# A two-layer hybrid decoder trunk: each engine's instruction order taken from a list schedule over the traced program

## The chip, the cores and the metric

The kernel runs on one core of one Trainium2 chip. A core has five engines that work side by side, each through its own queue of instructions: TensorE (PE) multiplies matrices and loads weights for it (PEld), VectorE (DVE) and ScalarE (ACT) work element by element, GpSimd (POOL) does a little elementwise work here, and SyncE (SP) issues the transfers between the chip's memory and the core's on-chip memory. Engines wait for one another through semaphores. The metric is the device time of one execution in microseconds (us), from the first to the last instruction and what lies around it; lower is better.

## The reference

One sequence of 256 tokens with 2048 features goes through two layers. Both modulate their input with adaLN, and end in a post-norm residual. Layer A is a Mamba-2 mixer (64 heads in 8 groups, one chunk of 256 tokens), layer B attends with three dilated windows to keys and values made from layer A's output. Cut to what matters:

```python
def reference(x, c, ada_w, ada_b, ln_g, ln_b, a_in_w, ..., kv_w, b_in_w, b_out_w):
    for layer in range(DEPTH):                                    # DEPTH = 2
        shift, scale, gate = _adaln(c, ada_w[layer], ada_b[layer])  # silu(c) @ w + b
        h = x * (1.0 + scale) + shift
        if layer < N_A_LAYERS:
            y = _ssd_mixer(h, ...)       # h @ in_w, conv, SiLU, chunked scan, gate, norm, @ out_w
        else:
            y = _dilated_mixer(h, k_sh, v_sh, b_in_w[0], b_out_w[0])
        x = _layer_norm(DEEPNORM_ALPHA * x + (1.0 + gate) * y, ln_g[layer], ln_b[layer])
        if layer == N_A_LAYERS - 1:
            k_sh, v_sh = _shared_kv(x, kv_w)
    return x
```

All inputs and the output are 32-bit floats.

## The kernel before

**Weights.** Every large weight comes in pieces of 512 KB, 128 partitions by 1024 columns. `load_piece` (line 85) issues the load into one of six buffers called `raw`. `split` (line 90) makes two tiles out of it: ScalarE rounds it to `whi` (line 93), VectorE subtracts to get the remainder `wlo` (line 95); there are four buffers of each. A product of two 32-bit matrices is then three matmuls in the faster format: high by high, high by low, low by high. `cm_piece` (lines 119 to 121) does it with the weights as the stationary operand and 256 tokens moving, `cm_wide` (151 and 152) with both parts of the activation in one matmul of 512 columns, `tm_mults` (172 to 174) with the activation stationary and 512 weight columns moving. Activations lie in the tile `actT`, split in the same manner.

**adaLN.** The modulation of 2048 features is a vector by matrix product. It runs on VectorE: `ada_dot` (line 237) multiplies a tile `araw` of 1 MB (128 outputs by 2048 inputs, loaded by `ada_load` at line 230) with `silu(c)` in `cb_` and sums along the row. There are 96 such dots: 32 for shift and scale of layer 0, 16 for its gate, 48 for layer 1. The last two groups are background work: `queue` and `background` put one in after every few pieces. `gate_out` (line 244) transposes a finished gate and writes it out.

**Stages.** (1) The first matmuls (line 425) spread `c` over all partitions, ScalarE takes its SiLU (426), VectorE makes two dots, and ScalarE and VectorE the first tile of `h` (384 to 386). While the other tiles of `h` come, TensorE works on pieces of ten different products, in an order that is written out by hand (lines 395 to 398): each product is begun on the tiles of `h` that exist, and its part sum is put aside (483 and 485). (2) For eight groups `product` makes `bc`, `xs` and `z`, `conv` does the convolution (303 to 308), `stage1`, `stage2` and `stage3` the scan of a group (L551 and L553 make decay factors, L562 transposes, L541 evicts scores, L592 and L584 multiply, L594 gates). (3) `y_tiles` transposes and splits the result (645 to 648), four chunks of the output projection follow, each with `residual` (663 to 665). (4) `ln_scale` computes the LayerNorm's factors in a chain of some fifteen small VectorE operations that ends in `nb` (677); lines 700 and 702 apply them in column chunks, block 0 on ScalarE, block 1 on VectorE; `x_tiles` transposes (715) and splits (718 to 720). (5) Keys and values, layer B's queries, attention (`attend`) and gate. (6) The last projection; its second half keeps all pieces split in memory, so that token block 0 ends before block 1, and block 0's norm and output (882 to 885) run beside block 1's matmuls.

**What sets the order.** Each engine executes its queue in order. The kernel is written with a framework that traces the program in Python, then gives each engine its queue, places tiles in buffers and adds the semaphores; of what is ready in its own simulation it takes what was traced first. Besides, a few places are pinned by hand: a list cell `pin[0]` and the `after` arguments hold an instruction, and `tc.issue_after(ins)` makes the instructions traced in its block come behind `ins` in their engine's queue. Dots are pinned behind the first h steps (line 436), behind the last split before group 1 (609) and before the wide key products (745); the splits after the LayerNorm are pinned behind `nb` (740 and 746).

Of the kernel before, what the change touches and what calls it, by code (L numbers as in the profile page):

```python
# [49 lines left out]
def trunk(ctx, tc, xT, x, c, par, cst, bias, lnrow, ada, wdt, win, wout, wkv, wk1, wbin, wbout, out):  # L50
# [38 lines left out]

    def split(raw, into=None, after=None):  # L90

        hi, lo = into or [wp.tile([P, 1024], F32R, name=n, bufs=4) for n in ("whi", "wlo")]
        S.activation(hi, raw, AF.Copy)  # L93
        with tc.issue_after(after) if after is not None else ExitStack():
            latest[0] = V.tensor_tensor(lo, raw, hi.bitcast(F32), op=ALU.subtract)  # L95
        return hi.rearrange("p (k n) -> p k n", k=2), lo.rearrange("p (k n) -> p k n", k=2)

    jobs, latest, pin = [], [None], [None]

# [8 lines left out]

    def cm_piece(src, q, ps, ahi, alo, k0=0, k1=KT, raw=None, after=None):


        hi, lo = split(load_piece(src[q]) if raw is None else raw, after=after)
        for k in range(2):
            kt = 2 * q + k
            for n in range(4):
                o = ps[n // 2][:, n % 2, :]
                c_ = slice(n * P, n * P + P)
                first = kt == k0 and n % 2 == 0
                T.matmul(o, hi[:, k, c_], ahi[:, kt, :], start=first, stop=False, skip_group_check=True)  # L119
                T.matmul(o, hi[:, k, c_], alo[:, kt, :], start=False, stop=False, skip_group_check=True)  # L120
                T.matmul(o, lo[:, k, c_], ahi[:, kt, :], start=False, stop=kt == k1 - 1, skip_group_check=True)  # L121

    def cm_quads(work, ahi, alo, pre=None, after=None):
        for q in range(KT // 2):
            if pre:
                pre(q)
            for src, ps in work:
                cm_piece(src, q, ps, ahi, alo, after=after if q == 0 else None)

# [103 lines left out]
    def ada_dot(layer, kind, ct, raw):  # L233

        j = KIND.index(kind)
        with tc.issue_after(pin[0]) if pin[0] is not None else ExitStack():
            V.scalar_tensor_tensor(raw, raw, 1.0, cb_, op0=ALU.mult, op1=ALU.mult,  # L237
                                   accum_out=mod[layer][:, ct, j:j + 1])

# [33 lines left out]
    with ExitStack() as cA:  # L273
# [14 lines left out]
        with ExitStack() as cS:  # L288
# [63 lines left out]
            with ExitStack() as c0:  # L352
# [15 lines left out]
                def h_step():  # L368
# [6 lines left out]
                    ada_dot(0, kind, kt, raw)  # L375
                    if kt > 1:
                        pin[0] = None
                    fetch()
# [53 lines left out]
                for _ in range(2):  # L432
                    for _ in range(2):
                        h_step()
                    while late:
                        pin[0] = late.pop()().ins
                    fetch_piece()
# [169 lines left out]
            for g in range(G - 1):  # L607
                if g == 1:
                    pin[0] = latest[0].ins
                    queue(wp1, [(0, "gate", kt) for kt in range(KT)])  # L610
                    jobs.append(lambda: gate_out(0))
                if g % 2 == 1:
                    product("bc", g + 1)
                product("xs", g + 1)
                if rs is not None:
                    stage3(g - 1, rs)
                st1 = stage1(g)
                if g < G - 2:
                    product("z", g + 1)
                rs = stage2(g, *st1)  # L620
# [46 lines left out]
        def ln_scale(blocks=(0, 1)):  # L667
# [8 lines left out]
            nb = sm.tile([P, n], F32, name=tag + "nb", bufs=1)  # L676
            last = V.scalar_tensor_tensor(nb, mv[:, :, 0], -1.0, r, op0=ALU.mult, op1=ALU.mult)
            return r, nb, last

# [14 lines left out]
        drain()  # L694
        r, nb, nb_last = ln_scale()
        for c0_, c1_ in ((0, 256), (256, 512), (512, 1024), (1024, 1536), (1536, 2048)):
# [39 lines left out]
    with ExitStack() as cL:  # L736
        pl = cL.enter_context(tc.tile_pool(name="pl", bufs=3))
        ex = cL.enter_context(tc.tile_pool(name="ex1", bufs=2, space=PSUM))
        ps = [acc_pair(), acc_pair(), acc_pair(ex)]
        cm_quads([(wkv[2 * g], ps[g]) for g in range(NG)], xhi, xlo, pre=ahead, after=nb_last.ins)  # L740
        for g in range(NG):
            evict_k(0, g, ps[g])

        R = (4, 9)
        pin[0] = latest[0].ins
        with tc.issue_after(nb_last.ins):
            queue(pl, cols1[16:])
            jobs.append(lambda: gate_out(1))
            for g in range(NG):
                for w in range(2):  # L750
                    cm_wide(wk1[2 * g + w], kk[1][:, g, 2 * w:2 * w + 2, :], rate=R)
            for hq in range(2):
                for g in range(NG):
                    ps = tm_chunk(wkv[6 + 2 * g + hq], hx, lx, rate=R)
                    for b in range(2):
                        S.activation(vt[hq][:, g, b, :], ps[b], AF.Copy)
            drain()

# [115 lines left out]
    for b in range(2):  # L874
        for n in range(2):
            for q in range(4):
                tm_mults(q, held[4 * n + q], ps[n], *og, 0, H, (b,))
            join(2 + n, ps[n][b], b)
        r, nb, _ = ln_scale((b,))
        for c in range(4):  # L880
# [3 lines left out]
            V.tensor_tensor(u[b][:, cs_], u[b][:, cs_], lnt[:, 1, cs_], op=ALU.add)  # L884
            nc.sync.dma_start(out[b * P:b * P + P, cs_], u[b][:, cs_])


# [85 lines left out]
```

## Time and profile before

| | |
|---|---|
| runs without the profiler | 1299.74 us median of 3, 1298.78 to 1300.66 |
| profiled execution, its span from first to last instruction | 1298.3 us |
| mean granted TensorE clock in it | 0.989 of full speed |
| moved by DMA | 334.82 MB, mean 258 GB/s |
| matmuls, weight loads | 7386 each |

The profile records one execution; its own time is the span of 1298.3 us, which is 1.4 us under the median of the runs. Its page gives each engine's busy time, then groups of equal instructions: line, engine, operation, output and input tiles, count, busy time, mean duration in ns, and the idle time of the engine before them with what ended it. Other views list who waited for whom, the instructions in order of time, and busy time, clock and DMA share by stretch. A busy TensorE is not yet one at its peak, since a matmul's end is modelled and overlaps the next. Times in the views count from the span's start.

### The profile page before, as it was taken

Reading aid. Unit: us, or ns where it says so; the run is one execution under the profiler, and the core shown is the slowest. Engines: PE = TensorE matmul, PEld = TensorE weight load, DVE = VectorE, ACT = ScalarE, POOL = GpSimd, SP = SyncE. Lnnn points to the kernel's source line nnn. Section 1 sums busy time; section 2 is a strip of 40 time slices with the busy share of each in tenths; the row PEclk is TensorE's granted clock in tenths of the full one; section 3 lists DMA queues with packets and bytes.
Section 4 is the critical chain, followed back from the end, with each engine's and each line's share of the span. In section 5 each row is a group of like instructions: output and inputs, shape, how many; then the busy total and the mean of one; then the engine's idle time right before and its main releaser. Section 6 shows DMA issues by size and latency. Waiting matters only on the chain.

```text
span 1298.3 us, 19349 instructions
## 1 busy us (share of the span) xinstructions
PE 1249.2 (96%) x7386; PEld 1097.9 (85%) x7386; DVE 1029.1 (79%) x1457; ACT 709.1 (55%) x1039; POOL 27.6 (2%) x20
## 2 busy tenths in 40 slices
PE   6999999999999999999999799999999999999995
PEld 4878988899899999778888699888887888888884
DVE  5888887899999778899765578888768747758687
ACT  3544457867687687864333444444435645445651
POOL 0000000000000000000000043000000000000000
PEclk9999999999999999999999899999999999999998
DMA  9999966697885546398977575999897754352461
GB/s 373 407 374 408 384 203 239 221 343 239 305 315 180 183 160 211 132 336 325 386 254 219 190 238 175 352 380 368 326 345 276 268 181 145 114 188 89 163 259 65
DMA packets 80449, 334.82 MB, mean 258 GB/s; under 512 B 9090, under 2 KB 9314, under 8 KB 67684
## 3 DMA queue, kind: packets, MB, share of 16 engines
q1 hardware_dynamic: 80356, 333.58, 71.2%
q8 instruction: 58, 0.95, 0.3%
q14 instruction: 35, 0.29, 0.1%
HBM read 331.37 MB, written 2.18 MB: 257 GB/s over the span
## 4 chain that ended last, share of the span: by engine, by line
PE 86%; DVE 9%; ACT 3%; issue 2%; DMA 1%; SPq 0%; DVEq 0%; ACTq 0%
PE acc L151 13%; PE acc L173 12%; PE acc L174 11%; PE acc L172 11%; PE acc L121 9%; PE acc L119 8%; PE acc L120 8%; PE acc L152 6%; DVE wlo L95 2%; DVE araw L237 2%; PE py L592 2%; PE aux L801 1%; ACT whi L93 1%; PE po L815 1%; PE po L825 1%
## 5 line engine op out<-in xcount | busy, mean ns | idle before, releaser
L95 DVE TENSOR_TENSOR wlo<-raw,whi 128x1024 fp32r<-128x1024 f32 x395 | 486.0, 1243 | 189.7 <-ACT whi L93 187.5
L93 ACT ACTIVATE whi<-raw 128x1024 fp32r<-128x1024 f32 x395 | 412.6, 1056 | 326.9 <-PE acc L174 141.6
L119 PE MATMUL acc<-actT,whi 128*128 128x256 f32 x960 | 274.9, 289 | 14.0 <-ACT actT L385 8.9
L173 PE MATMUL acc<-wlo,actT 128*128 128x512 f32 x704 | 276.7, 393 | 3.2 <-DVE wlo L95 3.1
L121 PE MATMUL acc<-actT,wlo 128*128 128x256 f32 x960 | 271.9, 287 | 4.5 <-DVE wlo L95 4.5
L120 PE MATMUL acc<-actT,whi 128*128 128x256 f32 x960 | 273.9, 287 | 0.0
L172 PE MATMUL acc<-whi,actT 128*128 128x512 f32 x704 | 272.2, 394 | 0.8 <-ACT actT L647 0.7
L151 PE MATMUL acc<-actT,whi 128*128 128x512 f32 x704 | 250.8, 398 | 0.0
L237 DVE SCALAR_TENSOR_TENSOR araw<-araw,cb__72 128x2048 f32<-128x2048 f32 x96 | 219.2, 2285 | 17.9 <-ACT cb__72 L426 9.2
L119 PEld LDWEIGHTS acc<-actT,whi 128*128 128x128 f32 x960 | 187.2, 196 | 17.8 <-ACT actT L385 10.6
L152 PE MATMUL acc<-actT,wlo 128*128 128x256 f32 x704 | 201.4, 286 | 0.0
L121 PEld LDWEIGHTS acc<-actT,wlo 128*128 128x128 f32 x960 | 185.9, 195 | 6.5 <-DVE wlo L95 6.4
L120 PEld LDWEIGHTS acc<-actT,whi 128*128 128x128 f32 x960 | 187.7, 195 | 0.3
L174 PE MATMUL acc<-whi,actT 128*128 128x512 f32 x448 | 175.0, 391 | 0.0
L173 PEld LDWEIGHTS acc<-wlo,actT 128*128 128x128 f32 x704 | 132.3, 188 | 33.4 <-DVE wlo L95 6.9
L151 PEld LDWEIGHTS acc<-actT,whi 128*128 128x128 f32 x704 | 132.3, 188 | 30.2
L172 PEld LDWEIGHTS acc<-whi,actT 128*128 128x128 f32 x704 | 131.8, 188 | 28.5 <-ACT actT L647 1.5
L152 PEld LDWEIGHTS acc<-actT,wlo 128*128 128x128 f32 x704 | 133.2, 189 | 0.5
L174 PE MATMUL acc<-whi,ylo 128*128 128x512 f32 x256 | 100.4, 393 | 0.0
L174 PEld LDWEIGHTS acc<-whi,actT 128*128 128x128 f32 x448 | 84.1, 188 | 17.1
L174 PEld LDWEIGHTS acc<-whi,ylo 128*128 128x128 f32 x256 | 48.0, 188 | 9.5
L551 ACT ACTIVATE seg<-cbc,cumT 128x128 f32<-128x128 f32 x128 | 40.5, 389 | 9.6 <-PE py L592 8.5
(206 smaller groups left out, 1089.0 us busy)
## 6 DMA issues: line engine op xcount, KB each, us to landing
araw<-in_ada SPq DMA_DIRECT2D x96, 1024.0 KB, 7.2
raw<-in_win SPq DMA_DIRECT2D x160, 512.0 KB, 5.1
raw<-in_wkv SPq DMA_DIRECT2D x72, 512.0 KB, 5.8
raw<-in_wout SPq DMA_DIRECT2D x64, 512.0 KB, 4.9
raw<-in_wbin SPq DMA_DIRECT2D x64, 512.0 KB, 3.6
raw<-in_wk SPq DMA_DIRECT2D x24, 512.0 KB, 8.4
cbc<-cumd SPq DMA_DIRECT2D x16, 512.0 KB, 5.2
raw<-in_wbout SPq DMA_DIRECT2D x16, 512.0 KB, 3.8
```

Source lines behind the costliest of these rows:

```text
L93: S.activation(hi, raw, AF.Copy)
L95: latest[0] = V.tensor_tensor(lo, raw, hi.bitcast(F32), op=ALU.subtract)
L119: T.matmul(o, hi[:, k, c_], ahi[:, kt, :], start=first, stop=False, skip_group_check=True)
L120: T.matmul(o, hi[:, k, c_], alo[:, kt, :], start=False, stop=False, skip_group_check=True)
L121: T.matmul(o, lo[:, k, c_], ahi[:, kt, :], start=False, stop=kt == k1 - 1, skip_group_check=True)
L151: T.matmul(ps[n], hi[:, k, c_], xp[:, kt], start=kt == 0, stop=False, skip_group_check=True)
L152: T.matmul(ps[n][:, 0, :], lo[:, k, c_], xhi[:, kt, :], start=False, stop=kt == KT - 1, skip_group_check=True)
L172: T.matmul(ps[b], h_, hi[:, k, :], start=kt == k0, stop=False)
L173: T.matmul(ps[b], h_, lo[:, k, :], start=False, stop=False)
L174: T.matmul(ps[b], l_, hi[:, k, :], start=False, stop=kt == k1 - 1)
L237: V.scalar_tensor_tensor(raw, raw, 1.0, cb_, op0=ALU.mult, op1=ALU.mult, accum_out=mod[layer][:, ct, j:j + 1])
L551: S.activation(seg[:, hh, b, :], cbc[:, hh, b, :], AF.Relu, bias=cumT[:, b, h0 + hh:h0 + hh + 1], scale=-1.0)
```

## The change

All pins go: `split`, `cm_piece` and `cm_quads` lose `after`, `ada_dot` loses `pin`, `ln_scale` no longer returns its last instruction, and the `issue_after` blocks fall away. What is computed, the tiles, the buffers and their counts stay as they are. After the program is traced, `arrange(tc)` runs, and then the framework makes the queues as before.

`graph` goes through the traced instructions and finds for each the ones it depends on, by overlap of what they read and write; `build` and `prepare` add the buffers of each tile name and the reuse of memory between pools. Tiles of one name get their buffers in the order of the program. `price` gives each instruction two durations: how long it holds its engine, and when its result is there. `forward` then plays the program: an engine that is free takes, of what is ready by then, the instruction with the smallest key; ScalarE avoids a change of its function table where another choice is near enough; VectorE and ScalarE may stay idle for a more urgent instruction that is about to become ready (`hold`). Transfers follow one another at 425 GB/s behind a latency of 2 us, at most eight at a time. `backward` computes from the played schedule how late each instruction may start, and that is the key of the next round. The first round's key is the program's order. Of six rounds the one with the shortest modelled time is kept, and `arrange` adds an edge without a semaphore from each instruction to the one before it on its engine, SyncE's transfers included.

```diff
-    def split(raw, into=None, after=None):
+    def split(raw, into=None):
...
         S.activation(hi, raw, AF.Copy)
-        with tc.issue_after(after) if after is not None else ExitStack():
-            latest[0] = V.tensor_tensor(lo, raw, hi.bitcast(F32), op=ALU.subtract)
+        V.tensor_tensor(lo, raw, hi.bitcast(F32), op=ALU.subtract)
...
-        with tc.issue_after(pin[0]) if pin[0] is not None else ExitStack():
-            V.scalar_tensor_tensor(raw, raw, 1.0, cb_, op0=ALU.mult, op1=ALU.mult,
-                                   accum_out=mod[layer][:, ct, j:j + 1])
+        V.scalar_tensor_tensor(raw, raw, 1.0, cb_, op0=ALU.mult, op1=ALU.mult,
+                               accum_out=mod[layer][:, ct, j:j + 1])
...
-        cm_quads([(wkv[2 * g], ps[g]) for g in range(NG)], xhi, xlo, pre=ahead, after=nb_last.ins)
+        cm_quads([(wkv[2 * g], ps[g]) for g in range(NG)], xhi, xlo, pre=ahead)
...
-        pin[0] = latest[0].ins
-        with tc.issue_after(nb_last.ins):
-            queue(pl, cols1[16:])
...
+        queue(pl, cols1[16:])
...
+def price(x, e):
+
+    outs, ins = _aps(x.outs), _aps(x.ins)
+    o = outs[0]
+    if e == "SP":
+        return 0.36, 0.0, None, _n(o) * list(o.ap)[0][1] * 4
+    if e == "PE":
+        n = _n(ins[0])
+        if "float32r" in str(ins[0].dtype):
+            return (n / 2400 + 0.0133 if n < 512 else 0.2268), 0.177 + n / 2400, None, 0
...
+    if e == "Activation":
+        f = str(x.func).split(".")[1]
+        d = (0.165 + n / 1190 if ps else 0.19 + n / 1175) + 0.085 * ptr
+        return d - 0.095, d, {"Silu": 1, "Exp": 2}.get(f), 0
...
+            d = 0.152 + n / 960 + 0.057 * ptr
+        return d - 0.083 + 0.08 * (len(outs) > 1), d + 0.08 * (len(outs) > 1), None, 0
...
+RATE, DMALAT, LANES = 425e3, 2.0, 8
...
+def forward(P, key, hold, penalty=1.3):
...
+        if v.e == "SP":
+            free["SP"] = t + v.occ
+            dmafree = max(dmafree, t + v.occ + DMALAT) + v.nb / RATE
+            fin[i] = dmafree
+            lanes.append(fin[i])
...
+        f, a = fut[e], avail[e]
+        while f and f[0][0] <= t + 1e-9:
+            r, k, i = heapq.heappop(f)
+            heapq.heappush(a, (k, i))
...
+        k, i = heapq.heappop(a)
+        if hold and e in ("DVE", "Activation") and f:
+            v = nodes[i]
+            lim = t + v.occ
+            urgent = [(r, kk, j) for r, kk, j in f if r < lim - 0.05 and kk < k and kk < lim + hold]
...
+        begin(i, t)
...
+def arrange(tc, rounds=ROUNDS):
+
+    ins = list(tc.nc.cur_bb.bb.instructions)
+    work = [x for x in ins if type(x).__name__ != "BassTilePoolBoundary"]
+    P = prepare(ins, tc.info.pools)
+    key, best = [float(v.i) for v in P[0]], None
+    for k in range(rounds):
+        start, fin, order, slotedge, _ = forward(P, key, 3.0 if k else 0.0)
+        if best is None or max(fin) < best[0]:
+            best = max(fin), order
+        key = backward(P, start, fin, order, slotedge, max(fin))[0]
+    last = {}
+    for i in best[1]:
+        e = P[0][i].e
+        if e in last:
+            tc.add_manual_dep(work[i], last[e].name, mybir.DependencyInfo(
+                mybir.DependencyClass.NoSync, mybir.DependencyReason.DATA), reason="order")
+        last[e] = work[i]
...
     with _tile.TileContext(nc) as tc:
         trunk(tc, out=out, **args)
+        arrange(tc)
```

More of the change, by code (lines that the diff above doesn't have):

```diff
@@ L107, in trunk, with cm_piece @@
     state = [0]
-    def cm_piece(src, q, ps, ahi, alo, k0=0, k1=KT, raw=None, after=None):
-        hi, lo = split(load_piece(src[q]) if raw is None else raw, after=after)
+    def cm_piece(src, q, ps, ahi, alo, k0=0, k1=KT, raw=None):
+        hi, lo = split(load_piece(src[q]) if raw is None else raw)
         for k in range(2):
@@ L121, in cm_piece, with cm_quads @@
                 T.matmul(o, lo[:, k, c_], ahi[:, kt, :], start=False, stop=kt == k1 - 1, skip_group_check=True)
-    def cm_quads(work, ahi, alo, pre=None, after=None):
+    def cm_quads(work, ahi, alo, pre=None):
         for q in range(KT // 2):
@@ L435, in trunk @@
                     while late:
-                        pin[0] = late.pop()().ins
+                        late.pop()()
                     fetch_piece()
```

400 lines of the change are left out of this document (382 added, 18 removed).

## The prediction

> **What bounds the kernel now.** I read the page first: who is busy, and what one instruction costs.
>
> ```profile
> span 1298.3 us, 19349 instructions
> ...
> PE 1249.2 (96%) x7386; PEld 1097.9 (85%) x7386; DVE 1029.1 (79%) x1457; ACT 709.1 (55%) x1039; POOL 27.6 (2%) x20
> ...
> L95 DVE TENSOR_TENSOR wlo<-raw,whi 128x1024 fp32r<-128x1024 f32 x395 | 486.0, 1243 | 189.7 <-ACT whi L93 187.5
> ...
> L237 DVE SCALAR_TENSOR_TENSOR araw<-araw,cb__72 128x2048 f32<-128x2048 f32 x96 | 219.2, 2285 | 17.9 <-ACT cb__72 L426 9.2
> ...
> araw<-in_ada SPq DMA_DIRECT2D x96, 1024.0 KB, 7.2
> ```
>
> TensorE is the bound: 1249.2 us of a span of 1298.3. No edit removes a matmul, so time can only come out of the moments in which TensorE waits, out of its slow clock, and out of the ends of the program. The next view is therefore the waits of TensorE, asked for by stretch: 17 to 160 us (layer 0's adaLN dots and first projection pieces), 160 to 730, 730 to 760 (the LayerNorm between the layers), the rest. The columns are who waited, for whom, us in total, times, longest.
>
> ```profile
> PE acc L119 <- ACT actT L385: 8.9, 2, 7.4
> PE acc L119 <- ACT whi L93: 3.6, 4, 1.6
> PE acc L121 <- DVE wlo L95: 2.4, 4, 1.4
> PE acc L173 <- DVE wlo L95: 0.7, 2, 0.3
> ...
> PE acc L121 <- DVE wlo L95: 2.1, 4, 0.7
> PE acc L173 <- DVE wlo L95: 1.9, 2, 1.4
> PE aux L562 <- ACT cb L541: 1.1, 1, 1.1
> PE aux L645 <- DVE ylo L648: 0.9, 1, 0.9
> PE acc L172 <- ACT actT L647: 0.7, 1, 0.7
> ...
> PE aux L715 <- ACT u L700: 5.7, 1, 5.7
> PE acc L119 <- ACT actT L718: 1.5, 1, 1.5
> ...
> PE acc L173 <- DVE wlo L95: 0.5, 1, 0.5
> ```
>
> The 7.4 in the first row is the wait for the first h tile, so 17 to 160 us holds 1.5 + 3.6 + 2.4 + 0.7 = 8.2 us. 160 to 730 us holds 6.7, the LayerNorm 7.2, all the rest 0.5. After 760 us there is almost nothing to win. The third view gives clock and DMA by stretch (busy us and count for PE, PEld, DVE, ACT, POOL, then granted clock, DMA share, GB/s):
>
> ```profile
> 0.00:17.00 17.00, 7.21 (x9) 2.53 (x9) 5.32 (x9) 5.62 (x9) 0.20 (x4) 1.00 0.85 326
> 37.20:40.60 3.40, 3.40 (x18) 3.40 (x17) 3.40 (x4) 1.66 (x3) 0.00 (x0) 0.50 0.99 412
> 40.60:85.00 44.40, 41.63 (x246) 35.51 (x245) 33.43 (x37) 21.73 (x30) 0.00 (x0) 1.00 0.99 396
> 85.00:88.40 3.40, 3.40 (x17) 3.40 (x18) 3.40 (x3) 1.36 (x2) 0.00 (x0) 0.50 0.89 283
> 88.40:160.00 71.60, 69.95 (x484) 65.29 (x484) 63.59 (x70) 36.19 (x46) 0.00 (x0) 1.00 0.99 396
> 180.00:540.00 360.00, 356.51 (x2469) 328.96 (x2468) 315.00 (x521) 273.06 (x448) 0.00 (x0) 1.00 0.66 229
> ```
>
> Two stretches of 3.4 us run at half clock, each a few us after a wait; half of 2 x 3.4 is another 3.4 us lost. But the DMA engines are at a share of 0.99 up to 160 us: that stage is bound by two resources at once.
>
> **Why order can matter.** The timeline shows what the waits have in common: an engine stands before an instruction that is not ready, while one that is ready, and that TensorE needs, is queued behind it.
>
> ```profile
> 81.32 1.29 ACT L485 ACTIVATE sz<-acc 128x512 f32<-128x512 f32 x2 [5.88 <-PE acc L174]
> 82.51 1.99 ACT L93 ACTIVATE whi<-raw 128x1024 fp32r<-128x1024 f32 x2
> 83.61 0.39 PE L119 MATMUL acc<-actT,whi 128*128 128x256 f32 x1 [1.63 <-ACT whi L93]
> ...
> 141.53 0.69 DVE L483 TENSOR_TENSOR y<-acc,y 128x512 f32<-128x512 f32 x1 [2.77 <-PE acc L121]
> ...
> 142.86 1.22 DVE L95 TENSOR_TENSOR wlo<-raw,whi 128x1024 fp32r<-128x1024 f32 x1
> ...
> 565.57 2.29 DVE L237 SCALAR_TENSOR_TENSOR araw<-araw,cb__72 128x2048 f32<-128x2048 f32 x1 [1.73 <-DMA araw<-in_ada]
> 567.78 0.87 DVE L648 SCALAR_TENSOR_TENSOR ylo<-aux,prm,actT 128x256 fp32r<-128x256 f32 x2
> ```
>
> ScalarE stood 5.88 us before an eviction (L485) and only then made the whi that TensorE lacked; the half-clock stretch from 85 follows. VectorE stood 2.77 us before L483 with a split behind it. At 565 us it gave 1.73 + 2.29 us to a dot that nobody needs soon, with ylo behind it.
>
> **The change part by part.** *Pins removed* (issue_after around L95 and L237): no instruction goes, cost nothing by itself, since the chain of edges orders more than they did. *Edges added*: one from each instruction to its predecessor on its engine. They carry no semaphore, so I expect the same 19349 instructions; the bounds for their own cost are 0 and, were each of the 1457 VectorE instructions 1 ns longer, 1.5 us; I take 0. *Prices*: the schedule is only as good as its durations. For a split it assumes 0.152 + 1024/960 = 1.219 us against the row's 1.243, for a dot 0.152 + 2048/960 = 2.285 against 2.285. Compute is priced within 2%. An ada load alone in the queue is priced 0.36 + 2.0 + 1048576/425000 = 4.8 us, the row says 7.2 at the median; transfers queue in the schedule too, so some of the 2.4 us is covered. *What moves*, by stage:
>
> 17 to 160 us: 8.2 + 3.4 = 11.6 us are lost to order. The cover is DMA: its idle share is 0.15 x 17 + 0.11 x 3.4 + 0.01 x (44.4 + 71.6) = 4.1 us. SP's own order matters here: it held two ada loads whose buffers were not free, and the next piece load (issued at 12.90) behind them:
>
> ```profile
> 6.28 6.58 SPq L230 DMA_DIRECT2D araw<-in_ada  x2
> ```
>
> Between 4.1 (bytes decide) and 11.6 (a higher rate is possible: 412 GB/s stands beside 396) I take 4.1, nearest to the share rows.
>
> 160 to 730 us: 6.7 us of waits. VectorE is busy 315.00 of 360 us in 180 to 540, so where it is full a split moved forward only makes another operation late. I leave 1.7 of the L121 waits and take 5.0. Rest after 760 us: 0.5.
>
> The LayerNorm:
>
> ```profile
> 738.13 1.22 DVE L95 TENSOR_TENSOR wlo<-raw,whi 128x1024 fp32r<-128x1024 f32 x1
> 738.25 3.21 ACT L700 ACTIVATE u<-u,m01nb,m01y 128x256 f32<-128x256 f32 x5 [3.98 <-DVE m01nb L677]
> 739.27 2.10 DVE L702 TENSOR_SCALAR u<-u,m01y,m01nb 128x256 f32<-128x256 f32 x5
> 741.36 1.00 ACT L718 ACTIVATE actT<-aux,prm 128x256 fp32r<-128x256 f32 x2
> ```
>
> A split precedes L702, and all five L700 precede the first L718. One 256-column L700 is 3.21/8 = 0.4 us. With L702 at 738.25, transposes at about 738.7 and L718 at about 739.2, the next matmuls come 2.2 us sooner; a 0.8 us L700 in progress can spoil a little: 2.0. What is late next is the chain from bn_aggr to nb, which no order shortens.
>
> The tail, after the last matmul:
>
> ```profile
> 1277.90 0.68 DVE L663 TENSOR_TENSOR actT<-acc,actT 128x512 f32<-128x512 f32 x1
> ...
> 1282.11 0.69 DVE L664 SCALAR_TENSOR_TENSOR u<-u,actT 128x512 f32<-128x512 f32 x1
> ...
> 1283.91 0.68 DVE L663 TENSOR_TENSOR actT<-acc,actT 128x512 f32<-128x512 f32 x1
> ...
> 1289.73 0.69 DVE L883 TENSOR_TENSOR u<-u,actT 128x512 f32<-128x512 f32 x1 [0.88 <-ACT u L882]
> ```
>
> Block 0's outputs hold back block 1's L664 by 4 us. But VectorE is the bound here and work put off must be done later; only its idle 0.88 us before L883 can be filled: 0.9.
>
> Sum: 4.1 + 5.0 + 0.5 + 2.0 + 0.9 = 12.5. The profiled span 1298.3 becomes 1285.8; it lies 1.4 under the median 1299.7 of the runs, so the forecast is **1287**.
>
> **Two rules of the Trainium skill.** The rows show half clock after waits of about 1.6 us. The Trainium skill ("TensorE: Matmul & The Clock Gate", What's actually happening) says the clock halves after an idle window of about 3.4 us; the length of the slow stretch agrees, the shorter wait does not. By that rule alone the 3.4 us would not be won, and only the fullest case below would shrink, to about 1277. Against the change speaks the same page (Architectural detail): ScalarE and VectorE are "strict FIFO", TensorE only pulls weight loads ahead. The 5.88 us before L485 agrees; a fixed order that guesses wrong pays the same way.
>
> **The rivals.** (a) *Forecast*, 1280 to 1294. (b) *The waits only move*: DMA and a full VectorE keep both long stages as they are; left are LayerNorm, rest and tail, 3.4 us: 1296, within 1294 to 1297. For it: shares 0.99 and 315 of 360. Against: 45 us of VectorE are free there. (c) *All goes*: 11.6 + 6.7 + 0.5 + 2.2 + 0.9 = 21.9, and each wait is really longer than its row, because a matmul's modelled 0.39 us outlasts the start-to-start 0.23 by 0.16; with some 24 waits, 3.8 more: 25.7, so 1274. Against: the DMA share. (d) *The change does not do what it says*: the first of its six rounds takes program order as urgency, and the best round by the model is kept; if that one wins, the order is nearly today's: 1300. (e) *Slower*: a dot placed at a time when its tile is believed landed, but lands up to 2.4 us later (7.2 against 4.8); VectorE stands, splits queue behind it, TensorE starves, as at 565 us. Place: the dots after 180 us. To lose the 12.5 and 2.6 more takes 15.1/2.4 = 6.3, so seven of 96 dots; eight give 1299.7 - 12.5 + 19.2 = 1306. Against: only 17.9 us of idle stand before all 96 dots now, and the schedule queues transfers.
>
> **How the numbers follow.** Chances: (a) 0.44, (b) 0.13, (c) 0.18, (d) 0.09, (e) 0.16. Faster is a + b + c = 0.75; within 0.2% (2.6 us, about what a measurement can tell from no change) 0.09; slower 0.16. The likeliest case alone has 1280 to 1294. The range goes down to 1272, below (c), and up to 1303, which leaves out most of (e).
>
> **What would show it.** Right: the same instruction count; TensorE's waits between 17 and 730 us well under 14.9 us; no row like L485 with 5.88 before whi; first L718 under 740 on this clock; half-clock stretches at 37 and 85 gone. Wrong: VectorE idle before L237 released by araw grown from 17.9; TensorE waits on wlo in more places than today; a tail over 16 us.

## The result, and the profile after

The changed kernel takes 1282.72 us, median of 4 runs (1281.55 to 1283.74). The kernel before took 1300.20 us (4 runs, 1298.78 to 1301.41) beside it. The ratio is 0.9867, with a 95% interval of 0.9853 to 0.9881. It is 17.5 us faster. The forecast was 1287.

The profiled execution took 1281.55 us, with a span of 1279.8 us. These are the lines of its page that answer to those shown of before (some line numbers moved by a few: L237 is now L236, L93 is L94).

```profile
span 1279.8 us, 19378 instructions
...
PE 1239.4 (97%) x7386; PEld 1095.2 (86%) x7386; DVE 1039.2 (81%) x1457; ACT 696.6 (54%) x1027; POOL 33.3 (3%) x20
...
PE 78%; DMA 12%; DVE 7%; ACT 1%; issue 1%; SPq 0%; DVEq 0%; ACTq 0%
...
L95 DVE TENSOR_TENSOR wlo<-raw,whi 128x1024 fp32r<-128x1024 f32 x395 | 488.9, 1244 | 176.5 <-ACT whi L94 175.2
...
L236 DVE SCALAR_TENSOR_TENSOR araw<-araw,cb__72 128x2048 f32<-128x2048 f32 x96 | 218.4, 2286 | 9.0 <-DMA araw<-in_ada 5.7
```

The same matmuls, splits and dots run for the same time each. What shrank is idle time: VectorE stands 9.0 us before its dots (17.9 before the change), and TensorE is busy for 97% of a shorter span. The chain that ended last now has 12% of DMA in it (1% before): up to 145.6 us it is transfers almost without a break.

The waits of TensorE in the changed kernel, by stretch: 17 to 160 us, then 160 to 730, then after 760 (who waited, for whom, us in total, times, longest).

```profile
PE acc L119 <- ACT actT L382: 7.4, 1, 7.4
PE acc L119 <- ACT whi L94: 3.9, 5, 2.0
PE acc L172 <- ACT whi L94: 1.0, 3, 0.5
PE acc L121 <- DVE wlo L95: 0.9, 2, 0.6
PE acc L173 <- DVE wlo L95: 0.6, 1, 0.6
...
PE aux L711 <- ACT u L696: 5.7, 1, 5.7
PE acc L119 <- ACT actT L714: 0.5, 1, 0.5
PE acc L172 <- ACT actT L643: 0.5, 1, 0.5
PE aux L641 <- DVE ylo L644: 0.5, 1, 0.5
PE py L589 <- DVE xd L561: 0.5, 1, 0.5
PE py L589 <- DVE seg L551: 0.4, 1, 0.4
PE aux L581 <- DVE xo L569: 0.2, 1, 0.2
...
PE acc L152 <- DVE wlo L95: 0.6, 2, 0.4
PE acc L121 <- DVE wlo L95: 0.5, 1, 0.5
```

Beside the first h tile (7.4 again), 17 to 160 us holds 6.4 us of waits (8.2 before). From 160 us to the LayerNorm it is 2.1 us (6.7 before), the LayerNorm's two rows are 6.2 (7.2), and the rest has 1.1 (0.5).

Clock and DMA by stretch in the changed kernel (columns as before: busy us and count of PE, PEld, DVE, ACT, POOL, then granted clock, DMA share, GB/s):

```profile
35.00:85.00 50.00, 48.45 (x308) 43.34 (x307) 45.99 (x50) 28.81 (x40) 0.00 (x0) 1.00 1.02 423
85.00:160.00 75.00, 72.50 (x494) 66.32 (x493) 70.11 (x77) 35.99 (x46) 0.00 (x0) 1.00 1.01 406
...
180.00:540.00 360.00, 358.15 (x2458) 329.87 (x2457) 320.24 (x511) 262.61 (x441) 0.00 (x0) 1.00 0.69 231
...
725.00:731.90 6.90, 4.64 (x20) 4.24 (x21) 6.08 (x17) 5.13 (x9) 0.72 (x1) 0.51 1.02 330
```

The half-clock stretches at 37 and 85 us are gone; one of 6.8 us is left, in the LayerNorm (10.2 us there before). The DMA engines moved 423 and 406 GB/s where they moved 396.

Where did the 18.5 us of span go? For each pair of successive matmuls I take start to start, less the undisturbed distance of that shape (0.227 us for 512 columns in L172 to L174, 0.120 for 256 columns in L119 to L121, and so on), and sum it by stage. That is the time that TensorE lost, to waits, slow clock and small gaps alike; it is good to about 1 us in a stage, since the distances are averages. They are the same for both kernels, so what is won is surer than the two levels.

| stage | lost before, us | lost after, us | won | predicted |
|---|---|---|---|---|
| up to 160 us | 25.5 | 20.4 | 5.1 | 4.1 |
| to the LayerNorm (730 before, 720 after) | 11.8 | 4.9 | 6.9 | 5.0 |
| LayerNorm, to 760 us | 10.9 | 8.7 | 2.2 | 2.0 |
| after 760 us | 4.3 | 1.5 | 2.8 | 0.5 |
| after the last matmul | 16.1 | 14.7 | 1.4 | 0.9 |
| sum | | | 18.4 | 12.5 |

The last 0.1 us is the first matmul, which starts that much sooner.

### The profile page after: what moved, and what is told of

Same layout as the page of the kernel before. It is cut to its first block, busy times and chain, and to the rows that moved or that the text cites. A ratio compares the mean times of both kernels' runs of the same rounds, so it can differ in the third digit from the quotient of the medians.

```text
span 1279.8 us, 19378 instructions
## 1 busy us (share of the span) xinstructions
PE 1239.4 (97%) x7386; PEld 1095.2 (86%) x7386; DVE 1039.2 (81%) x1457; ACT 696.6 (54%) x1027; POOL 33.3 (3%) x20
## 4 chain that ended last, share of the span: by engine, by line
PE 78%; DMA 12%; DVE 7%; ACT 1%; issue 1%; SPq 0%; DVEq 0%; ACTq 0%
PE acc L151 12%; PE acc L174 11%; PE acc L173 11%; PE acc L172 11%; PE acc L152 6%; DMA raw<-in_win 6%; PE acc L119 6%; PE acc L121 6%; PE acc L120 6%; DMA araw<-in_ada 5%; DVE wlo L95 2%; PE py L589 1%; DVE araw L236 1%; PE aux L795 1%; PE po L819 1%
## 5 line engine op out<-in xcount | busy, mean ns | idle before, releaser
L95 DVE TENSOR_TENSOR wlo<-raw,whi 128x1024 fp32r<-128x1024 f32 x395 | 488.9, 1244 | 176.5 <-ACT whi L94 175.2
L94 ACT ACTIVATE whi<-raw 128x1024 fp32r<-128x1024 f32 x395 | 417.1, 1057 | 382.1 <-PE acc L174 178.6
L119 PE MATMUL acc<-actT,whi 128*128 128x256 f32 x960 | 273.6, 288 | 11.8 <-ACT actT L382 7.4
L173 PE MATMUL acc<-wlo,actT 128*128 128x512 f32 x704 | 276.4, 393 | 0.6 <-DVE wlo L95 0.6
L172 PE MATMUL acc<-whi,actT 128*128 128x512 f32 x704 | 274.8, 393 | 1.6 <-ACT whi L94 1.0
L121 PE MATMUL acc<-actT,wlo 128*128 128x256 f32 x960 | 270.5, 285 | 1.4 <-DVE wlo L95 1.4
L236 DVE SCALAR_TENSOR_TENSOR araw<-araw,cb__72 128x2048 f32<-128x2048 f32 x96 | 218.4, 2286 | 9.0 <-DMA araw<-in_ada 5.7
L119 PEld LDWEIGHTS acc<-actT,whi 128*128 128x128 f32 x960 | 185.2, 194 | 15.7 <-ACT actT L382 9.0
L121 PEld LDWEIGHTS acc<-actT,wlo 128*128 128x128 f32 x960 | 184.0, 193 | 2.3 <-DVE wlo L95 2.0
L174 PE MATMUL acc<-whi,actT 128*128 128x512 f32 x448 | 175.1, 391 | 0.0
L172 PEld LDWEIGHTS acc<-whi,actT 128*128 128x128 f32 x704 | 131.9, 188 | 30.1 <-ACT whi L94 2.8
L173 PEld LDWEIGHTS acc<-wlo,actT 128*128 128x128 f32 x704 | 132.3, 188 | 27.5 <-DVE wlo L95 1.1
L174 PE MATMUL acc<-whi,ylo 128*128 128x512 f32 x256 | 100.8, 394 | 0.0
L174 PEld LDWEIGHTS acc<-whi,actT 128*128 128x128 f32 x448 | 84.1, 188 | 17.5 <-issue 0.5
L174 PEld LDWEIGHTS acc<-whi,ylo 128*128 128x128 f32 x256 | 48.1, 188 | 9.4
L305 DVE SCALAR_TENSOR_TENSOR cacc<-acc,prm,cacc 128x255 f32<-128x255 f32 (+2 forms) x96 | 43.7, 475 | 2.7 <-ACT cacc L302 2.3
```

What stands on the lines that cost most here:

```text
L172: T.matmul(ps[b], h_, hi[:, k, :], start=kt == k0, stop=False)
L173: T.matmul(ps[b], h_, lo[:, k, :], start=False, stop=False)
L174: T.matmul(ps[b], l_, hi[:, k, :], start=False, stop=kt == k1 - 1)
L305: V.scalar_tensor_tensor(acc[:, o:], ps[:, :L - o], w[:, j:j + 1], acc[:, o:], op0=ALU.mult, op1=ALU.add)
```

## The experiments

The theory after the result: the win is the order itself, and two features of the schedule carry it, the urgency that `backward` works out and the look-ahead that lets an engine stay idle for something more urgent. The rivals: that taking off the pins freed the framework's own order (then no edges are needed); that only SyncE's or only TensorE's order counts; that the schedule would do without its look-ahead. And rival (e) of the prediction, the dot that stands before a tile that has not landed, was still to be found: the changed kernel hardly shows it, so the question was what keeps it away.

All times are medians beside the kernel before on the same chip (1300.9 to 1301.4 us there, 1300.2 beside the changed kernel), so a difference between runs of different rounds is good to about 1 us.

| run | edit to the changed kernel | us (lowest to highest) | ratio to before, 95% |
|---|---|---|---|
| e1 | no edges | 1306.51 (1304.63 to 1308.02) | 1.0040 [1.0029, 1.0051] |
| e2 | program order as urgency | 1328.89 (1326.58 to 1329.15) | 1.0204 [1.0189, 1.0219] |
| e3 | no look-ahead | 1313.48 (1309.83 to 1315.56) | 1.0087 [1.0066, 1.0107] |
| e4 | edges up to the LayerNorm alone | 1294.58 (1292.92 to 1296.37) | 0.9945 [0.9930, 0.9960] |
| e5 | no edges on TensorE | 1292.83 (1291.90 to 1294.60) | 0.9937 [0.9913, 0.9961] |
| e6 | no edges on SyncE | 1335.77 (1334.71 to 1338.35) | 1.0269 [1.0244, 1.0294] |
| e7 | GpSimd's work on VectorE | 1285.48 (1281.13 to 1288.45) | 0.9873 [0.9849, 0.9898] |
| e8 | e3 and e7 together | 1304.68 (1298.70 to 1310.04) | 1.0024 [1.0006, 1.0042] |
| e9 | look-ahead in the LayerNorm alone | 1306.88 (1302.80 to 1308.61) | 1.0041 [1.0024, 1.0058] |
| e10 | e3, landing priced 2.4 us later | 1299.26 (1295.17 to 1302.95) | 0.9988 [0.9974, 1.0003] |
| e11 | landing priced 2.4 us later | 1290.92 (1287.92 to 1293.81) | 0.9922 [0.9905, 0.9940] |
| e12 | e7 and e11 together | 1283.10 (1280.07 to 1286.27) | 0.9863 [0.9842, 0.9884] |

### e1: the pins gone, no edges

```diff
     with _tile.TileContext(nc) as tc:
         trunk(tc, out=out, **args)
-        arrange(tc)
```

> The pins are gone, no edge is added: the framework's own order. Theory U (the urgent-first order is the gain): the gain is lost, about 1300 us, or up to 1310 if the pins had earned something; waits of TensorE between 17 and 730 us at 14.9 us or more again. Rival P (the hand-made pins did harm, and dropping them is the gain): at most 1288 us.

It is slower than before: 1306.5. VectorE in the LayerNorm (timeline: start us, us, engine, line):

```profile
737.03 1.23 DVE L95 TENSOR_TENSOR wlo<-raw,whi 128x1024 fp32r<-128x1024 f32 x1
738.18 0.68 DVE L659 TENSOR_TENSOR u<-acc,gt 128x512 f32<-128x512 f32 x1
738.78 1.22 DVE L95 TENSOR_TENSOR wlo<-raw,whi 128x1024 fp32r<-128x1024 f32 x1
```

Two splits stand in the chain that ends in `nb`, which is what the pins had kept out; TensorE waits 7.6 us for `u` there, not 5.7. So the pins had earned some 5 us. From start to start TensorE loses 3.5 us more in the LayerNorm than before and 3.2 more between 160 us and there. The edges make that up and bring 17.5 on top: from e1 to the changed kernel it is 1306.5 - 1282.7 = 23.8 us. The rival that the pins were in the way falls.

### e2: program order as the urgency

```diff
-ROUNDS = 6
+ROUNDS = 1
```

> One round only: the played program takes, of what is ready, what was traced first; no urgency, no holding. Rival M (what matters is that readiness is played with true durations, so that nobody stands before an instruction that is not ready): within 3 us of the changed kernel's 1282.7. Theory U: rows like the 5.88 us before L485 vanish, but dots of 2.29 us still go ahead of splits, so between a third and two thirds of the 17.5 us, 1288 to 1295.

One round means that the key is the program's order, and no look-ahead is used. It took 1328.9 us, slower than any theory had it. In its LayerNorm (timeline of VectorE):

```profile
745.22 2.29 DVE L236 SCALAR_TENSOR_TENSOR araw<-araw,cb__72 128x2048 f32<-128x2048 f32 x1 [3.35 <-DMA araw<-in_ada]
```

This is rival (e) as it was written down: a dot fixed in the order where its tile was believed landed, 3.35 us of VectorE idle, and the chain to `nb` behind it. TensorE's wait for `u` is 15.4 us. A list schedule is not an improvement by being one. Beside e3, which has no look-ahead either, the urgency is worth 1328.9 - 1313.5 = 15.4 us; program order with look-ahead was not run.

### e3: no look-ahead

```diff
-        start, fin, order, slotedge, _ = forward(P, key, 3.0 if k else 0.0)
+        start, fin, order, slotedge, _ = forward(P, key, 0.0)
```

> Six rounds with urgency, but an engine never stays idle for a more urgent instruction that is about to be ready. Theory U without holding is the whole gain: 1281 to 1285. Theory H (holding matters, because a dot holds VectorE 2.29 us, longer than the 1.06 us that ScalarE needs for the next whi): a wait of up to 1.2 us comes back at some of the 96 dots, 1286 to 1293.

1313.5 us, 30.8 above the changed kernel, from one number. VectorE's timeline in the LayerNorm, without look-ahead:

```profile
731.76 0.16 DVE L208 TENSOR_TENSOR m01y<-magic,m01s 128x2 int32<-128x2 int32 x1
735.30 2.29 DVE L236 SCALAR_TENSOR_TENSOR araw<-araw,cb__72 128x2048 f32<-128x2048 f32 x1 [3.38 <-DMA araw<-in_ada]
...
737.52 0.15 DVE L211 TENSOR_TENSOR m01t<-m01y 128x2 f32<-128x2 f32 x1
737.72 2.29 DVE L236 SCALAR_TENSOR_TENSOR araw<-araw,cb__72 128x2048 f32<-128x2048 f32 x1
...
739.94 0.16 DVE L212 SCALAR_TENSOR_TENSOR m01t<-m01t,m01ve 128x2 f32<-128x2 f32 x1
```

In the changed kernel L211 and L212 start 0.20 us apart, at 724.12 and 724.32. Each small operation of the chain needs the result of the one before, and by `price` that comes some 0.1 us after the engine is free for another. In that moment nothing urgent is ready, so the rule "of those that are ready, the most urgent" takes a dot of 2.29 us. With the look-ahead VectorE stays idle for that 0.1 us. Over the whole run VectorE waits 35.7 us for ada tiles in 26 places (changed kernel: 5.7 us in 8). From start to start, TensorE loses 9.8 us more in the LayerNorm than in the changed kernel and 16.0 more from there to 900 us, so the timeline above is not all of it.

### e4, e5, e6: a part of the edges

```diff
+    cut = sum(type(x).__name__ != "BassTilePoolBoundary" for x in ins[:mark[0]])
...
     for i in best[1]:
         e = P[0][i].e
+        if i >= cut:
+            continue
```

> Edges only between instructions traced before the LayerNorm's factors; behind it the framework's order, and there too without pins. If the gain sums up by stages as the trace has it (5.1 us up to 160 us, 6.9 from there to the LayerNorm, about 6 behind): 1288 to 1290. If what lies behind the LayerNorm had needed its pins: above 1293. If the early gain is given back at the LayerNorm: above 1297.

`mark` is set in front of `ln_scale()`. With the edges up to there alone, 1294.6 us: 6.7 us of the gain are there and 11.9 are missing (1294.6 - 1282.7). The wait for `u` is 7.6 us, as without any edges. The 11.9 are not the second half's alone: in the profiled execution a wait of 1.29 us at 232 us is followed by 10.2 us at half clock, which is 5.1 us that the changed kernel did not lose there. So the times say that both halves count, and not how much of each. The trace says more: with no edges from the LayerNorm on, TensorE loses 5.4 us more there, 2.9 more after 900 us, and the tail is 1.3 longer.

e5 and e6 put this in the loop instead, with "PE" or with "SP":

```diff
+        if e == "PE":
+            continue
```

> The same schedule, but TensorE gets no edges and takes what the framework gives it. Theory V (the order on VectorE, ScalarE and SyncE carries the gain; TensorE is nearly forced by its data): 1280 to 1286. Rival T (TensorE's own order carries it, as at the 1.1 us before L562): 1287 to 1296.

1292.8 us: TensorE's own order is worth 10.1 us. It waits 4.1 us at 541 us (L172 for the tile of L643), where the changed kernel has 0.5, and after 900 us it loses 2.9 us more.

> The same schedule, but SyncE gets no edges: transfers are issued in the framework's order. If SyncE's order makes the 5 us of the first 160 us (423 GB/s now against 396 before between 35 and 85 us): 1286 to 1290, and the rate falls back to about 396. If the buffers alone decide when a load can go: 1280 to 1285. If another order makes VectorE stand before dots whose tile was to land earlier: above 1293.

1335.8 us, the slowest of all. Waits in this run, VectorE's and then TensorE's:

```profile
DVE araw L236 <- DMA araw<-in_ada: 55.2, 33, 3.7
```

```profile
PE acc L173 <- DVE wlo L95: 16.7, 13, 3.6
```

The compute engines keep an order made for other landing times. VectorE stands 55.2 us before 33 dots, the splits queue behind them, and TensorE waits 16.7 us for `wlo` in L173 alone. It is rival (e) at full size, and what brings it on is that the transfers are out of step with the rest. The rate from 35 to 85 us is 413 GB/s (423 in the changed kernel), and 359 from 85 to 160 us (406). A part of the schedule can be worse than none.

### e7, e8: GpSimd's work moved to VectorE

In the changed kernel's trace some splits took twice as long as the others. VectorE, then GpSimd:

```profile
788.68 2.31 DVE L95 TENSOR_TENSOR wlo<-raw,whi 128x1024 fp32r<-128x1024 f32 x1
...
792.35 2.31 DVE L95 TENSOR_TENSOR wlo<-raw,whi 128x1024 fp32r<-128x1024 f32 x1
...
796.01 1.21 DVE L95 TENSOR_TENSOR wlo<-raw,whi 128x1024 fp32r<-128x1024 f32 x1
```

```profile
785.06 7.08 POOL L766 TENSOR_TENSOR u<-u,lnr 128x512 f32<-128x512 f32 x2 [9.34 <-issue]
792.10 3.70 POOL L767 TENSOR_TENSOR u<-u,lnr 128x512 f32<-128x512 f32 x2
```

The splits that start beside the operations of L766 and L767 take 2.31 us, the next one, behind them, 1.21. So these two lines went to VectorE:

```diff
-                PO.tensor_tensor(u[b][:, cs_], u[b][:, cs_], lnr[0], op=ALU.mult)
-                PO.tensor_tensor(u[b][:, cs_], u[b][:, cs_], lnr[1], op=ALU.add)
+                V.tensor_tensor(u[b][:, cs_], u[b][:, cs_], lnr[0], op=ALU.mult)
+                V.tensor_tensor(u[b][:, cs_], u[b][:, cs_], lnr[1], op=ALU.add)
```

> The changed kernel with its 16 elementwise operations of GpSimd (the LayerNorm's gain and bias) on VectorE instead. In the trace a split takes 2.31 us beside a GpSimd operation against 1.22 without, which no price knows, and TensorE loses about 2.2 us in waits between 780 and 820 us. Theory C (that contention is the loss): 1279 to 1281.5. Rival: the 16 operations, about 11 us at 0.69 each, come in the way of splits: 1283 to 1286.

1285.5 us, not to be told from the changed kernel by the ratios, but with a wide spread. TensorE's loss between 780 and 820 us went from 2.2 us to 0, as it should. It came back at another place: a wait of 1.3 us at 232 us (VectorE had stood 2.2 us before two dots there, 0.85 in the changed kernel), and then half clock:

```profile
235.00:245.20 10.20, 10.17 (x34) 8.26 (x34) 8.21 (x11) 4.73 (x11) 0.00 (x0) 0.50 0.68 226
```

Half of the 10.2 us at a clock of 0.50 is lost, 5.1 us.

> No holding, and no GpSimd operations. Without holding alone 1313.5 us was measured, of which the trace puts some 16 us between 760 and 900 us, where GpSimd works, and some 10 at the LayerNorm. If contention makes the 16: 1297 to 1303. If missing holding makes them, through dots put before splits: 1309 to 1314.

The time lies between the two readings, nearer the first. Without look-ahead the same move is worth 1313.5 - 1304.7 = 8.8 us: of the 17.4 us that TensorE loses in e3 between 760 and 900 us, 7.1 are left. What GpSimd slows depends on what the order puts beside it.

### e9, e10: what is wrong without look-ahead

```diff
-        if hold and e in ("DVE", "Activation") and f:
+        if hold and 700 < t < 740 and e in ("DVE", "Activation") and f:
```

> The look-ahead of 3 us (an engine lets a ready instruction wait for a more urgent one that is about to be ready) is kept only in the stretch of the LayerNorm, from 700 to 740 us of the schedule's own clock. Without it anywhere the time was 1313.5 us, and 10 us of that were put down to the two dots between the small operations of the LayerNorm. If that reading is right, these 10 us come back and the rest stays: 1303 us (1298 to 1307), TensorE's wait for u between 5.5 and 8 us, VectorE's wait for ada tiles still over 25 us. If the LayerNorm only showed a delay that was made elsewhere, the time stays within 1308 to 1316. If the look-ahead is worth its whole effect there, the time is that of the changed kernel, 1283.

1306.9 us, at the very end of the first reading's range: 6.6 us came back, not 10. The LayerNorm's wait is 5.7 again, as in the changed kernel, and VectorE's wait for ada tiles is still large:

```profile
DVE araw L236 <- DMA araw<-in_ada: 25.9, 24, 4.6
```

From start to start TensorE gets 9.4 of the 9.8 us in the LayerNorm back, and loses 3.2 more ahead of it, where 10.2 us at half clock follow a wait of 2.0 us at 235 us. So the LayerNorm is one place among several.

```diff
-RATE, DMALAT, LANES = 425e3, 2.0, 8
+RATE, DMALAT, LANES = 425e3, 4.4, 8
```

> No look-ahead anywhere, but the fixed part of a load priced at 4.4 us and not at 2.0, so that an ada tile alone in the queue is believed landed at 7.2 us, the median of the trace. Theory one, the wrong price of the landing makes VectorE stand: its wait for ada tiles falls from 35.7 us to under 10, no dot stands between the small operations of the LayerNorm, TensorE's wait for u is under 8 us, and the time is 1285 to 1297. Theory two, taking what is ready is itself the fault and the price does not matter: still over 20 us of waits for ada tiles or over 10 us of wait for u, 1306 to 1316.

On top of e3's edit. 1299.3 us lies between the two theories. VectorE's wait for ada tiles is a third of e3's, and no dot stands in the chain to `nb`:

```profile
DVE araw L236 <- DMA araw<-in_ada: 11.8, 14, 2.2
```

```profile
PE acc L119 <- ACT actT L382: 12.3, 1, 12.3
PE aux L711 <- ACT u L696: 7.6, 1, 7.6
```

14.2 of the 30.8 us came back with the price alone; 16.5 are missing. They are not simply the look-ahead's: with this price in both kernels it is worth 8.3 us (1299.3 here, 1290.9 in e11), with the old price 30.8. The two act on each other. Two splits stand between the statistics of the second block (wait 7.6). The first h tile comes 4.9 us later (12.3 for 7.4): a dot goes ahead of L241, which starts at 16.76 and not at 14.65, and the rest of that delay is on ScalarE. It hardly counts, since TensorE's loss up to 160 us is 21.1 us in all (20.4 in the changed kernel). What it loses more in this trace lies in the LayerNorm (4.7 us) and between 760 and 820 us, beside GpSimd's work (4.8). Both theories hold a part.

### e11, e12: can the right price better the changed kernel?

> The changed kernel, look-ahead kept, with the fixed part of a load at 4.4 us. If the rest of the changed kernel's loss has the wrong price in it: VectorE's wait for ada tiles under 3 us (5.7 before the edit), no dot waits for its tile at 215 to 232 us, 1277 to 1281. If the look-ahead had covered it already: within 0.2% of the changed kernel, 1281 to 1285. If pricing every load too late makes the transfers start in a worse order in the first 160 us: 1286 to 1292, with the loss of TensorE up to 160 us over 23 us.

The edit of e10's diff, with the look-ahead kept: 1290.9 us, 8.2 slower than the changed kernel. The time is in the third range but not for its reason: TensorE's loss up to 160 us is 16.9 us, less than the 20.4 of the changed kernel. VectorE's wait for ada tiles did not fall, it rose to 12.2 us. The loss sits at 220 to 240 us (6.6 us, half clock after a wait of 1.6) and at 760 to 820 us (8.4), beside GpSimd's work: two dots there now take 3.37 us, where none did in the changed kernel. VectorE and GpSimd in e11:

```profile
771.73 2.31 DVE L95 TENSOR_TENSOR wlo<-raw,whi 128x1024 fp32r<-128x1024 f32 x1
773.96 3.37 DVE L236 SCALAR_TENSOR_TENSOR araw<-araw,cb__72 128x2048 f32<-128x2048 f32 x1
```

```profile
772.92 5.54 POOL L767 TENSOR_TENSOR u<-u,lnr 128x512 f32<-128x512 f32 x2
```

> The same price, and the four columns of the residual's scale and offset on VectorE and not on GpSimd. With them on VectorE alone the runs lay from 1281.1 to 1288.5, and the profiled one had 10 us at half clock from 235 us behind two dots that waited 2.2 us for their tiles. If those two dots are the cause of the spread: no half clock before the LayerNorm, waits for ada tiles under 3 us, a spread under 4 us, 1278 (1275 to 1282). If the spread has another cause: 1281 to 1289 again.

1283.1 us. The same stretch in e11 and in e12, from the view by stretch:

```profile
760.00:820.00 60.00, 54.53 (x416) 52.36 (x415) 59.34 (x57) 25.86 (x32) 18.89 (x8) 0.97 0.89 331
```

```profile
760.00:820.00 60.00, 60.00 (x452) 57.47 (x451) 59.40 (x67) 29.25 (x38) 0.00 (x0) 1.00 0.99 383
```

With GpSimd's 16 operations on VectorE, TensorE is busy 60.00 of 60 us and not 54.53, although VectorE has more to do: that is most of the 7.8 us between the two runs. (The traced executions lie 13.7 us apart; of the two only e11's has the half clock at 230 us.) The spread did not go, though: two runs took 1280.1 and 1280.9 at a mean clock of 0.993 and 0.992, two took 1285.3 and 1286.3 at 0.989. The difference of 0.004 of 1280 us is 5.1 us, one half-clock stretch of 10.2 us. So the spread stays without the two waits of e7. But the waits for ada tiles are 9.4 us and not under 3, 4.7 of them before one dot at 216 us, so the first reading was not put to its test. TensorE still waits about 1.4 us at 228 us. That this wait halves the clock in some executions and not in others would fit the four times; the one execution of e12 that was traced has no half clock there, and the cause of the spread is not shown. No version of mine beats the changed kernel by more than the intervals: e12 has 0.9863 [0.9842, 0.9884] beside 0.9867 [0.9853, 0.9881].

## Why the prediction was right, and where its sizes were off

The forecast was 1287 within 1280 to 1294, the time is 1282.7: case (a), by the mechanism given. The 4.3 us by which it is below, and the 6.0 us between 12.5 and the 18.5 of the span, are terms that were set too small.

**Up to 160 us: 4.1, measured 5.1.** The step that failed is the cap. It took the idle share of the DMA engines as all that order could win, at 396 GB/s, and chose it over the higher rate that one row showed (412). The rate rose to 423 and 406, so a share of 0.99 did not mean that no more could be moved. The bytes do bound the stage: the chain is transfers up to 145.6 us, ScalarE now waits 30.0 us in 20 places for weights that have not landed (in no place before), and TensorE's waits fell only from 8.2 to 6.4 us. That the sum came within 1 us is partly luck: 1.8 us of waits and 3.4 us of clock were won, and nothing in the idle share of the DMA engines says so. The 3.4 us of half clock went completely. Two pieces of that chain (start us, us), and ScalarE's row of waits from 17 to 160 us:

```profile
24.76 14.95 DMA raw<-in_win
39.77 14.89 DMA araw<-in_ada
...
ACT whi L94 <- DMA raw<-in_win: 30.0, 20, 8.9
```

**160 to 730 us: 5.0, measured 6.9.** I left 1.7 us of the waits on L121 because VectorE seemed full at 315.00 of 360 us. It now has 320.24 us of work in the same stretch, and none of those waits is left. The rows fell by 4.6 us (6.7 to 2.1), the loss from start to start by 6.9. The remark in case (c), that a wait is 0.16 us longer than its row, makes at most 1.4 of these 2.3 us (nine waits); the rest lies in gaps that the rows don't list.

**LayerNorm: 2.0, measured 2.2, of another make.** VectorE and ScalarE in the changed kernel:

```profile
725.88 0.16 DVE L673 SCALAR_TENSOR_TENSOR m01nb<-m01mv,m01y 128x2 f32<-128x2 f32 x1
726.08 0.74 DVE L698 TENSOR_SCALAR u<-u,m01y,m01nb 128x256 f32<-128x256 f32 x2
726.73 1.22 DVE L95 TENSOR_TENSOR wlo<-raw,whi 128x1024 fp32r<-128x1024 f32 x1
...
726.08 1.80 ACT L696 ACTIVATE u<-u,m01nb,m01y 128x256 f32<-128x256 f32 x3 [3.98 <-DVE m01nb L673]
727.78 1.00 ACT L714 ACTIVATE actT<-aux,prm 128x256 fp32r<-128x256 f32 x2
```

The split went behind L698, and L714 in front of the last L696, as forecast. From the first L696 to the first L714 it is now 1.70 us (738.25 to 741.36 before: 3.11), 1.4 sooner and not 2.2, because three L696 still precede it and one is of 512 columns. The row of L714's wait fell from 1.5 to 0.5 us. The rest came from the clock, at half for 6.8 us and not 10.2, which the forecast had left out: TensorE works for 4.6 us of that stretch and not 6.6, so it loses 1.0 us less. The chain to `nb` stays, 5.7 us, as it said.

**After 760 us: 0.5, measured 2.8.** This is the largest miss for its size. The forecast read the view of waits, which lists 0.5 there. The trace of before loses 4.3 us from start to start there: 0.7 in one place (L173 at 1000 us, the row of 0.5), the rest in pieces under 0.25 us, which that view doesn't list. Most of these lie in the stretch of the attention, around its small matmuls (products of `kk` and `qq`, transposes of `sc`), and those alone come 2.8 us closer together in the changed kernel. TensorE's order does it, about half by who follows whom: a small matmul has a wide one of the projection behind it 60 times and not 48, and that one starts 0.03 us behind it, where another small one starts 0.11 us (128 columns) or 0.22 (256) behind. Four traces separate it: without TensorE's edges (e5), or with none behind the LayerNorm (e4), the small ones lie as far apart as before, within 0.1 us; with TensorE's edges and the same prices (e6, e7) they are as close as in the changed kernel. The wide matmuls between them lose 1.5 us more, so the attention as a whole wins 1.5. Shorter gaps and waits before and behind it win some 3.5, and 2.2 us between 780 and 820 us, beside GpSimd's work, are new.

**Tail: 0.9, measured 1.4.** VectorE in the changed kernel:

```profile
1265.14 0.69 DVE L659 TENSOR_TENSOR actT<-acc,actT 128x512 f32<-128x512 f32 x1
...
1270.01 1.29 DVE L878 TENSOR_TENSOR u<-u,actT 128x512 f32<-128x512 f32 x2
```

The last L659 starts right behind the last matmul (1265.1), not 1.6 us later (1283.91 beside 1282.3), and block 0's L878 fills the gap of 0.88 us behind `nb`. The work that was put off costs some of it back.

**The pins** cost "nothing by itself": by e1 they had earned 5 us, and the edges do cover them. **The same 19349 instructions** was wrong: 29 more. The trace has 41 more semaphore instructions, 36 of them on SyncE, and 12 fewer loads of ScalarE's function tables (27 and not 39, 1.28 us each). Fewer such loads are not what decides: e5 and e6 have 27 as well, at 1292.8 and 1335.8 us. The matmuls and VectorE's instructions are the same in number. That the edges cost nothing is borne out by the durations: a split takes 1244 ns on average (1243 before), a dot 2286 (2285).

**The rivals.** (b) and (c) were the right mechanisms in the wrong amounts. (d) was wrong in its price: it held that the first round would give nearly today's order and 1300 us, but it gives 1328.9 (e2). (e) had the right place, price and mechanism; what it lacked was what decides. An ada load alone in the queue is priced 2.4 us under the median of the trace, and without look-ahead that price is worth 14.2 us (e10); but with the look-ahead, which the prediction named in no term, the same correction costs 8.2 us (e11), so there the early price does no harm: VectorE waits 5.7 us for tiles in the changed kernel, 35.7 without. That the diff itself holds a guard against the case should have been weighed there.

## What to carry to other kernels

Here a greedy "most urgent of those that are ready" needed a look-ahead: a chain of 0.2 us operations leaves holes into which a 2.3 us operation falls, and that rule alone made the kernel slower than before (1313.5 us; 1299.3, the same as before, with loads priced 2.4 us later). An order fixed for all engines is one thing with the order of the transfers; with SyncE left out, the rest was worse than no order (1335.8 beside 1306.5). When reading a profile, set start to start against the undisturbed distance as well as the list of waits: gaps too short to be listed made 3 us here after 760 us.

## What the runs showed of the hardware

**VectorE beside GpSimd.** Most splits that run beside GpSimd's 512-column operations take 2.31 us and not 1.22 (eight of ten in the changed kernel), and a dot 3.37 and not 2.29. Moving GpSimd's operations to VectorE won 7.8 us from e11 to e12, and nothing from the changed kernel to e7. The Trainium skill ("SBUF — State Buffer", SBUF: two separate sides) says that the two engines share a port pair that is locked for a whole instruction, and that an operation of VectorE with two inputs in the core's memory contends for it; splits and dots have two such inputs, and the trace agrees that they are held. The schedule prices GpSimd's work as if it ran alone.

**The clock.** Waits are taken here from start to start, less the undisturbed distance. The clock halved for 10.2 us after waits of TensorE of 1.32 us (e7) and 1.57 us (e11), but not after 1.43 (e12) and 1.37 (e10). In the kernel before it halved for 3.4 us after 1.8 us at 33 and 82 us, but not after 1.6 us at 25, 142 and 165 us. The Trainium skill ("TensorE: Matmul & The Clock Gate", What's actually happening) gives an idle window of about 3.4 us that runs freely. The stretches up to the last matmul are whole multiples of 3.41 us long (3.41, 6.83, 10.24), which agrees. A shorter wait was enough, which doesn't; that the phase decides which wait is enough would fit the page, and no run shows it.

**The transfers** went at 423 GB/s over 50 us in the new order, where 396 at a share of 0.99 had looked like the cap. SyncE's order is not all of it: with SyncE in the framework's order (e6) the same 50 us have 413. What sets the rate no run shows.
